# A two-layer hybrid decoder: first up tile with eight plain products, norm sums on VectorE, six banks for the output projection, another order of queues

## The chip, the cores and the metric

The kernel runs on one core of a Trainium2 chip. The metric is the device time of one execution in microseconds. The kernel before took 2763.81 us, the median of three runs (2761.84 to 2765.71).

The engines are named as the profile names them: PE is TensorE (matmuls), DVE is VectorE, ACT is ScalarE, POOL is GpSimd; SP issues most DMAs.

## The reference

One inference step over a prompt of 1024 tokens and eight sample sequences of 8 tokens with shared weights; the kernel treats them as 1088 columns of width 1024. Layer 0 mixes with an S5 state-space model, layer 1 with forgetting attention (FoX) over new and paged keys and values. Both have a cross-attention to a memory of 256 tokens and a squared-ReLU MLP of width 4096.

```
z = rmsnorm(h, norm_mix[i]) @ w_in[i]               # 768 main columns, 256 memory queries
y_mem = memory_attend(z[..., 768:], mem_k[i], mem_v[i])
layer 0: y = s5 scan of z (48 groups of 16 channels, 64 states)
         g = gelu(y);  y_main = g * sigmoid(g @ w_glu + b_glu)
layer 1: y_main = fox_attend(z, cumulative log-forget, past and new k, v)
h = h + concat(y_main, y_mem) @ w_out[i]
h = h + relu(rmsnorm(h, norm_mlp[i]) @ w_up[i])**2 @ w_down[i]
```

Outputs are the final norm of h, the S5 states, the memory and shared keys and values and the log-forget values, all float32.

## The kernel before

Every matmul operand is split into a rounded high part H and a rest L; a product is three matmuls (H·H, H·L, L·H; `mm3`, L209). The function `split` makes H on ScalarE (L221) and L, by a subtraction with two inputs, on an engine that is handed in (L222: VectorE, or GpSimd). The 1088 columns lie in four chunks of 272, and most matmuls are 128x272.

**S5 and GLU, layer 0.** The S5 work runs in units; GpSimd makes part of each (L1131, L1138, L1140, L1141), VectorE the rest (L1129, L1132, L1137), and a unit's result goes by ScalarE's queue (L1151) into the DRAM buffers yscr[0] to yscr[5]. SP loads them back in another layout (L1215), each is split for all four chunks, and only then the GLU's matmuls over six slices k can end. `past_rows` gathers past log-forget rows with 16 indirect DMAs on GpSimd (L1227), `past_sums` scans them on VectorE (L1233 to L1237) and stores them to fpast on SP (L1238). Their calls stand in the GLU's loop over chunks (c == 1, c == 3), but the scheduler puts instructions where it reckons that their engine is free, so they lie among the S5 units. Memory attention's 16 units are woven into the GLU's matmuls; their probabilities are scaled on GpSimd or VectorE (L734).

**Output projection and norm.** `out_proj` makes eight output tiles m for each chunk, first m = 0, 1 over all chunks, then m = 2 to 7 over all chunks, each tile of 24 matmuls in one of two PSUM banks (`dbank`); the addition to the residual (L329) frees it. When a chunk is whole, `mlp_norm` takes its sum of squares (`rms_sums`, L260, L261, on GpSimd; for the last chunk on VectorE), two ticks later its scale (L272 to L275), the product (L441; the last chunk L438, eight times), and then the MLP's operands.

**MLP up.** An up tile is a 2x2 block product in Winograd's form: seven block products instead of eight (`seven`), each of 12 matmuls per group of columns. Chunks 0 and 1 are group 0, chunks 2 and 3 are group 1; within a group the two chunks are the two column blocks. The form needs seven operands for a group of columns (`operands`: four split sums and differences, L356 to L363, and three plain ones) and seven for a tile of weights (`weight_ops`: four sums on GpSimd, L386 to L392, and seven splits). For the first tile (j = 14) group 0 and group 1 are made one after the other, and the weights' splits but the first lie on GpSimd; for the other 15 tiles both groups are made together and all splits lie on VectorE. Differences held back (`held`) and norms put off (`defer`, `tick`) come later in the program.

The order of instructions on each engine is set by a scheduler that reads the program in the order in which it is written, keeps data dependences and the edges of `issue_after` (`after(ins)`), and otherwise chooses by its own estimate of when things are ready.

## Time and profile before

| | us |
|---|---|
| median of three runs | 2763.81 |
| the profiled execution | 2768.41 |
| its span | 2766.5 |
| TensorE busy | 2569.8 (93%) |
| VectorE busy | 1963.9 (71%) |
| ScalarE busy | 1253.5 (45%) |
| GpSimd busy | 1310.3 (47%) |

The profile is of one execution; the row of the profiled execution is its whole time, the span is from its first to its last instruction. A timeline row gives the start, the duration, the engine, the line, the tile written and read, how many instructions it covers, and in brackets how long the engine was idle before it and what ended that. In a table by windows the count in brackets behind an engine's busy time is that of its instructions; PEclk is the granted clock of TensorE, 1.00 for 2.4 GHz and 0.50 for 1.2 GHz.

In time: S5 until about 298 us, GLU and memory attention until 410, output projection of layer 0 until 500, its MLP until 1235, layer 1's projections and attention until 1935, its output projection until 2020, its MLP to the end.

### The profile page before, as it was taken

What the parts mean: (1) busy time and instruction counts of PE and PEld (TensorE: products, weight loads), DVE (VectorE), ACT (ScalarE), POOL (GpSimd) and SP (SyncE); (2) the same over time, 40 slices, a digit from 0 to 9 for tenths busy, and PEclk for the clock granted to TensorE, in tenths of its full rate; (3) what the DMA queues carried; (4) which work ended last, traced back from release to release, by engine and by line L of the source; (5) the groups of instructions that cost most, each with busy time, mean ns of one, the idle gap of its engine ahead of it and who ended that gap; (6) DMA issues with size and microseconds to landing.
All of it is one profiled execution on the core that took longest, in us unless ns stands there. A gap on an engine that the chain in (4) does not pass through costs nothing.

```text
span 2766.5 us, 54068 instructions
## 1 busy us (share of the span) xinstructions
PE 2569.8 (93%) x20345; PEld 2401.5 (87%) x20345; DVE 1963.9 (71%) x3337; ACT 1253.5 (45%) x2592; POOL 1310.3 (47%) x1184
## 2 busy tenths in 40 slices
PE   6888799799998999999999999998979999899998
PEld 5877689799997999999889867776979999799998
DVE  8898654888886777784323278885488878577776
ACT  5433453566663222244322377774356666322224
...
GB/s 200 110 110 155 120 133 80 85 219 231 240 224 314 226 257 279 180 167 102 146 260 220 273 300 307 306 294 198 64 80 224 237 234 224 322 227 257 274 176 66
DMA packets 242283, 561.65 MB, mean 203 GB/s; under 512 B 54053, under 2 KB 129382, under 8 KB 224614
## 3 DMA queue, kind: packets, MB, share of 16 engines
...
q0 software_dynamic: 512, 0.79, 0.1%
...
## 4 chain that ended last, share of the span: by engine, by line
PE 44%; DVE 22%; DMA 13%; POOL 9%; issue 6%; ACT 5%; SPq 1%; POOLq 0%; ACTq 0%; DVEq 0%
PE banks L209 42%; DMA hops<-plain 7%; DVE rounded L222 6%; POOL plain L574 4%; DVE plain L222 3%; POOL plain L392 1%; ACT plain L221 1%; PE banks L1599 1%; DMA rounded<-hmid 1%; DVE plain L536 1%; POOL plain L582 1%; DMA hcnv<-plain 1%; ACT rounded L221 1%; POOL plain L388 1%; POOL plain L386 1%
## 5 line engine op out<-in xcount | busy, mean ns | idle before, releaser
L209 PE MATMUL banks<-rounded 128*128 128x272 f32 (+3 forms) x11168 | 1561.3, 296 | 108.6 <-ACT rounded L221 28.2
L209 PEld LDWEIGHTS banks<-rounded 128*128 128x128 f32 x11168 | 1465.6, 192 | 156.3 <-ACT rounded L221 31.9
L221 ACT ACTIVATE rounded<-plain 128x512 fp32r<-128x512 f32 (+5 forms) x571 | 379.8, 677 | 587.1 <-PE banks L209 420.9
L222 DVE TENSOR_TENSOR rounded<-plain,rounded 128x512 fp32r<-128x512 f32 (+4 forms) x500 | 509.0, 1022 | 119.8 <-ACT rounded L221 114.1
L209 PE MATMUL banks<-mlp,rounded 128*128 128x272 f32 x3840 | 524.1, 291 | 17.6 <-ACT rounded L221 11.1
L209 PEld LDWEIGHTS banks<-mlp,rounded 128*128 128x128 f32 x3840 | 499.9, 190 | 23.3 <-ACT rounded L221 12.3
L386 POOL TENSOR_TENSOR plain<-plain 128x512 f32<-128x512 f32 x60 | 91.5, 1525 | 488.9 <-DVE rounded L222 488.7
L574 POOL TENSOR_TENSOR plain<-plain,flex 128x544 f32<-128x544 f32 x192 | 290.8, 1523 | 42.3 <-DVE plain L573 39.8
L222 DVE TENSOR_TENSOR plain<-plain 128x544 fp32r<-128x544 f32 x212 | 165.0, 788 | 87.3 <-ACT plain L221 84.1
L221 ACT ACTIVATE plain<-plain 128x544 fp32r<-128x544 f32 x212 | 137.5, 649 | 145.1 <-DMA hops<-plain 123.5
L573 DVE TENSOR_TENSOR plain<-banks,plain 128x544 f32<-128x544 f32 x192 | 137.8, 718 | 54.7 <-PE banks L209 50.9
L392 POOL TENSOR_TENSOR plain<-plain 128x512 f32<-128x512 f32 x60 | 118.2, 1970 | 88.4 <-DVE rounded L222 87.9
L222 POOL TENSOR_TENSOR rounded<-plain,rounded 64x512 fp32r<-64x512 f32 (+4 forms) x71 | 112.0, 1586 | 76.9 <-ACT rounded L221 69.5
L537 ACT ACTIVATE plain<-plain 128x544 f32<-128x544 f32 (+1 forms) x136 | 85.3, 628 | 79.2 <-DVE plain L536 78.8
L209 PE MATMUL banks<-layer 128*32 128x256 f32 (+3 forms) x1152 | 111.8, 371 | 8.1 <-ACT layer L1422 3.9
L222 POOL TENSOR_TENSOR rounded<-flex,rounded 128x544 fp32r<-128x544 f32 (+7 forms) x100 | 67.3, 681 | 86.7 <-ACT rounded L221 74.0
L209 PE MATMUL banks<-flexr,rounded 128*128 128x272 f32 x768 | 108.3, 290 | 0.0
L209 PEld LDWEIGHTS banks<-flexr,rounded 128*128 128x128 f32 x768 | 101.9, 190 | 0.0
L536 DVE TENSOR_TENSOR plain<-banks,plain 128x544 f32<-128x544 f32 (+1 forms) x136 | 92.9, 683 | 5.3 <-PE banks L209 4.8
L221 ACT ACTIVATE rounded<-banks 128x512 fp32r<-128x512 f32 (+2 forms) x136 | 75.0, 559 | 46.4 <-PE banks L1599 32.7
L222 DVE TENSOR_TENSOR rounded<-banks,rounded 128x512 fp32r<-128x512 f32 (+2 forms) x136 | 85.9, 636 | 14.1 <-ACT rounded L221 12.2
L260 POOL TENSOR_TENSOR flex<-flex 128x544 f32<-128x544 f32 x18 | 27.6, 1533 | 138.9 <-ACT flex L258 90.9
...
## 6 DMA issues: line engine op xcount, KB each, us to landing
...
plain<-in_cache_kT SPq DMA_DIRECT2D x128, 384.0 KB
layer<-in_cache_v SPq DMA_DIRECT2D x128, 384.0 KB
...
```

The source lines that it names most:

```text
L209: PE.matmul(out, a, b, start=first, stop=last)
L221: S.activation(H, src, AF.Copy)
L222: e.tensor_tensor(L, src, H.bitcast(F32), op=ALU.subtract)
L386: G.tensor_tensor(a22, a21, a22, op=ALU.add)
L388: G.tensor_tensor(a11, a22, a11, op=ALU.subtract)
L392: G.tensor_tensor(a12, a12, a11, op=ALU.subtract)
L536: V.tensor_tensor(x, ps, u, op=ALU.add)
L537: S.activation(x, x, AF.Relu)
L573: V.tensor_tensor(h, ps, h, op=ALU.add)
L574: G.tensor_tensor(h, h, u, op=ALU.add)
L582: G.tensor_tensor(hc, hc, hr[:, m, :], op=ALU.add)
L1599: PE.transpose(tb[:, k, 128 * i:128 * i + 128], p[i][:, 2 * c + k, :], ident)
```

## The change

- First up tile, group 1: four output blocks as plain sums of two block products each (eight products, 96 matmuls, for seven, 84). Its operands for them are the plain halves of chunks 2 and 3; the first tile's weights get an eighth split (slot 7, `put(7, a21)`). The sums and differences of group 1 that the later tiles need are made afterwards (`held.pop()()`). The second up tile too is now made in two groups.
- `rms_sums` on VectorE for all chunks; the operand splits and the first weights' splits that lay on GpSimd go to VectorE.
- Output projection: six banks in turn. Tiles in the order m = 0, 1 for chunks 0 to 2; m = 2, 3 for chunk 0; m = 0, 1 for chunk 3; m = 4 to 7 for chunk 0; then m = 2 to 7 for chunks 1, 2, 3.
- Order: the loads of x, w_out and the page indices come behind the last yscr load on SP; the gathers behind the GLU's y sums of chunk 0 on GpSimd, the multiplication of the page indices beside them; the past sums behind VectorE's products of chunk 2; the hcnv stores in one order with the loads of `hops` (not shown).

The diff, cut to its core:

```diff
@@ -252,7 +252,7 @@
-    def rms_sums(h, w, e=G, ring=sq):
+    def rms_sums(h, w, e=V, ring=sq):
@@ -314,21 +314,40 @@
-    def out_proj(ys, w, hs, done):
+    def out_proj(ys, w, hs, done, ins=None):
...
-        def load(src, shape):
-            m, src = src
-            return wall(src, shape, to=more[2 * m - 12:2 * m - 10] if m > 5 else None)
...
-        for g, n in ((0, 2), (2, 6)):
-            def ev(i, c, ps, w_, g=g):
-                r = hs[c][:, g + i, :]
-                V.tensor_tensor(r, ps, r, op=ALU.add)
...
-            dense([(m, w[m]) for m in range(g, g + n)], ys, ev, load, done=(lambda c: done(hs[c], c)) if g else None)
+        obank = Banks([0, 1, 2, 3, 4, 5])
+        W = {}
...
+        def load(ms):
+            with after(ins):
+                for m in ms:
+                    W[m] = wall(w[m], [128, 8, 128], to=more[2 * m - 12:2 * m - 10] if m > 5 else None)
...
+        def tiles(ms, c):
+            (xH, xL), n = ys[c], CH[c][1]
+            for m in ms:
+                H, L = W[m]
+                ps = obank([128, 512])
+                for k in range(8):
+                    mm3(ps[:, :n], H[:, k, :], L[:, k, :], xH[:, k, :], xL[:, k, :], k == 0, k == 7)
+                r = hs[c][:, m, :]
+                V.tensor_tensor(r, ps[:, :n], r, op=ALU.add)
+                tick()
...
+        load(range(4))
+        for c in range(3):
+            tiles((0, 1), c)
+        tiles((2, 3), 0)
+        tiles((0, 1), 3)
+        load(range(4, 8))
+        tiles(range(4, 8), 0)
+        done(hs[0], 0)
+        for c in range(1, NC):
+            tiles(range(2, 8), c)
+            done(hs[c], c)
@@ -346,7 +365,7 @@
-    def operands(b11, b12, b21, b22, extra, put, which=(0, 1, 2, 6)):
+    def operands(b11, b12, b21, b22, extra, put, which=(0, 1, 2, 5, 6)):
@@ -359,7 +378,8 @@
-            put(5, b22)
+            if 5 in which:
+                put(5, b22)
@@ -367,7 +387,7 @@
-    def weight_ops(src, cells, sh, e=V):
+    def weight_ops(src, cells, sh, more=None):
@@ -379,10 +399,13 @@
         def put(i, x):
-            split(r[i][:, 0], r[i][:, 1], x, e if i else V)
+            split(r[i][:, 0], r[i][:, 1], x)
...
         put(6, a22)
+        if more:
+            r.append(wr[more].at([128, 2, *sh], F32R))
+            put(7, a21)
@@ -427,7 +450,7 @@
-        s1 = rms_sums(h, w, V if last else G)
+        s1 = rms_sums(h, w)
@@ -449,23 +472,22 @@
-            extra = (nt0, setA[1])[g].at([128, 4, w]) if c % 2 else None
...
-            def put_of(g):
-                def put(i, t):
-                    o = xop(i, g)
-                    split(o[:, 0], o[:, 1], t, G if i in (2, 6) and not last else V)
-                return put
+            def put(i, t):
+                o = xop(i, g)
+                split(o[:, 0], o[:, 1], t)
...
-                operands(*b, extra, put_of(g), (0, 2))
+                operands(*b, None, put, (0, 2))
             elif not last:
-                operands(*b, extra, put_of(g), (1,))
-                held.append(lambda: operands(*b, extra, put_of(g), (6,)))
+                operands(*b, nt0.at([128, 4, w]), put, (1, 5))
+                held.append(lambda: operands(*b, None, put, (6,)))
             else:
                 held.pop()()
-                operands(*b, extra, put_of(g), (1, 6))
+                put(6, b[1])
+                put(5, b[3])
+                held.append(lambda: operands(*b, setA[0].at([128, 4, w]), put, (1, 6)))
@@ -474,12 +496,21 @@
-        def up_weights(j, e=V):
+        def up_weights(j, more=None):
-                              lambda r: (r[:, 0, 0:4], r[:, 0, 4:8], r[:, 1, 0:4], r[:, 1, 4:8]), [4, 128], e)
+                              lambda r: (r[:, 0, 0:4], r[:, 0, 4:8], r[:, 1, 0:4], r[:, 1, 4:8]), [4, 128], more)
@@ -524,13 +546,17 @@
-        W = up_weights(14, G)
+        assert turn["w"] % 3 == 0
+        W = up_weights(14, 7)
...
-            for gs in (slice(0, 1), slice(1, 2)) if n == 0 else (slice(0, 2),):
+            for gs in (slice(0, 1), slice(1, 2)) if n < 2 else (slice(0, 2),):
+                if n == 0 and gs.start:
+                    continue
...
                 def out(m, n, ps, u):
@@ -539,8 +565,20 @@
-                if gs.stop == 1:
-                    flush()
+            if n == 0:
...
+                flush()
+                for m, c in ((1, 0), (0, 0), (1, 1), (0, 1)):
+                    turn["bank"] = (turn["bank"] + 1) % 3
+                    ps = banks[:, 1024 * turn["bank"]:1024 * turn["bank"] + CN]
+                    for i in range(2):
+                        a, x = W[((0, 2), (7, 6))[m][i]], xop(((0, 2), (6, 5))[c][i], 1)
+                        for k in range(4):
+                            mm3(ps, a[:, 0, k, :], a[:, 1, k, :], x[:, 0, k, :], x[:, 1, k, :], i + k == 0, i + k == 4)
+                    t = q[m][c][:, 1]
+                    S.activation(t, ps, AF.Relu)
+                    S.activation(t, t, AF.Square)
+                held.pop()()
@@ -1212,17 +1250,18 @@
-        SY.dma_start(out=zs, in_=yscr[q].rearrange("(t c) g j -> (c g) t j", c=16))
+        zi = SY.dma_start(out=zs, in_=yscr[q].rearrange("(t c) g j -> (c g) t j", c=16))
...
-    SY.dma_start(out=pidx, in_=I["page_rows"])
-    SY.dma_start(out=hrow, in_=I["head_rows"])
-    V.tensor_scalar(pidx, pidx, 12.0, hrow[:, 0:1], op0=ALU.mult, op1=ALU.add)
+    with after(zi):
+        SY.dma_start(out=pidx, in_=I["page_rows"])
+        SY.dma_start(out=hrow, in_=I["head_rows"])
...
     def past_rows():
+        G.tensor_scalar(pidx, pidx, 12.0, hrow[:, 0:1], op0=ALU.mult, op1=ALU.add)
@@ -1240,9 +1279,11 @@
         if c == 1:
-            past_rows()
+            with after(gi):
+                past_rows()
         if c == 3:
-            past_sums()
+            with after(vi):
+                past_sums()
@@ -1254,8 +1295,8 @@
-            G.tensor_tensor(y, xH[:, m, :].bitcast(F32), xL[:, m, :].bitcast(F32), op=ALU.add)
-            V.scalar_tensor_tensor(y, t, 1.0, y, op0=ALU.add, op1=ALU.mult)
+            gi = G.tensor_tensor(y, xH[:, m, :].bitcast(F32), xL[:, m, :].bitcast(F32), op=ALU.add)
+            vi = V.scalar_tensor_tensor(y, t, 1.0, y, op0=ALU.add, op1=ALU.mult)
@@ -1267,10 +1308,10 @@
-    hs = [load_x(c) for c in range(NC)]
+    hs = [load_x(c, zi) for c in range(NC)]
         load_ym(0, c, 208 if c == NC - 1 else None)
-    out_proj(yx, I["w_out"][0], hs, lambda h, c: mlp_norm(h, c, 2))
+    out_proj(yx, I["w_out"][0], hs, lambda h, c: mlp_norm(h, c, 2), zi)
```

On SP's queue, from the last but one yscr load to the last, before:

```order
L1215 DMA plain<-yscr_135 128x8x136
L1209 DMA plain<-in_w_glu 128x768 x5
L1238 DMA fpast<-plain 96x1024 x2
L671 DMA plain<-in_cmk 128x512
L1190 DMA out_s5f<-prep_150 128x432
L671 DMA plain<-in_cmk 128x512
L197 DMA plain<-in_w_out 128x1024
L1215 DMA plain<-yscr_136 128x8x136
```

There the fpast stores (L1238), waiting for past sums, have ten later transfers behind them. After:

```order
L1253 DMA plain<-yscr_135 128x8x136
L694 DMA plain<-qmscr_86 128x2x64
L1253 DMA plain<-yscr_136 128x8x136
L1259 DMA plain<-in_page_rows 96x16
L1228 DMA out_s5f<-prep_150 128x432
L1260 DMA plain<-in_head_rows 96x1
L197 DMA plain<-in_w_out 128x1024
```

The last yscr load (yscr_136) moved ahead of the memory cache, w_out and the fpast stores.

On GpSimd's queue, the last S5 unit and the GLU's first y sums (L1257, after L1298; L1131 is L1169 after, L1138 is L1176), before:

```order
L1227 DMA plain<-in_logf_rows,plain 96x128 x4
L1131 TENSOR_TENSOR plain<-plain 128x512
L1138 TENSOR_TENSOR flex_69<-plain 64x2x128 x2
L1140 TENSOR_TENSOR prep_150<-plain 128x2
L1141 TENSOR_TENSOR prep_150<-plain 128x2
L1257 TENSOR_TENSOR plain<-rounded 128x272 x2
```

The last unit's first sum (L1131) has four gathers ahead of it. After:

```order
L1179 TENSOR_TENSOR prep_150<-plain 128x2
L1169 TENSOR_TENSOR plain<-plain 128x512
L1176 TENSOR_TENSOR flex_69<-plain 64x2x128 x2
L1178 TENSOR_TENSOR prep_150<-plain 128x2
L1179 TENSOR_TENSOR prep_150<-plain 128x2
L222 TENSOR_TENSOR rounded<-plain,rounded 128x768 x2
L1298 TENSOR_TENSOR plain<-rounded 128x272 x2
```

There the two last units follow each other, and no gather stands between.

On VectorE at the end of layer 0's output projection, from the last addition (L337) to the second tile, after (L434, L438, L442 and L562 take products out of PSUM, L375 to L383 are the differences):

```order
L337 TENSOR_TENSOR plain<-banks,plain 128x272
L222 TENSOR_TENSOR rounded<-plain,rounded 128x512
L275 TENSOR_TENSOR flex_69<-flex_69 128x272
L260 TENSOR_TENSOR flex_69<-flex_69 128x544
L464 TENSOR_TENSOR plain<-plain,flex_69 128x2176
L562 TENSOR_TENSOR plain<-banks,plain 128x272
L261 TENSOR_TENSOR flex_69<-flex_69 128x272
L434 TENSOR_TENSOR plain<-banks,plain 128x272
L438 TENSOR_TENSOR plain<-banks,plain 128x272
L562 TENSOR_TENSOR plain<-banks,plain 128x272 x2
L442 TENSOR_TENSOR plain<-banks,plain 128x272
```

These are the last addition, chunk 2's product and the first products of the tile. The next on VectorE, with chunk 3's norm:

```order
L222 TENSOR_TENSOR rounded<-plain,rounded 128x1088
L272 TENSOR_TENSOR flex_69<-flex_69 128x272
L562 TENSOR_TENSOR plain<-banks,plain 128x272
L222 TENSOR_TENSOR rounded<-plain,rounded 128x1088
L273 SCALAR_TENSOR_TENSOR flex_69<-banks,flex_69 128x272
L274 TENSOR_SCALAR flex_69<-flex_69 128x272
L275 TENSOR_TENSOR flex_69<-flex_69 128x272
L461 SCALAR_TENSOR_TENSOR plain<-plain,flex_69 128x272 x8
L375 TENSOR_TENSOR plain<-plain 128x1088
L222 TENSOR_TENSOR flexr_4581<-plain,flexr_4581 128x1088
L376 TENSOR_TENSOR plain<-plain 128x1088
L222 TENSOR_TENSOR flexr_4580<-plain,flexr_4580 128x1088
```

The second split into flexr ends the operands of the first tile; L379, two splits of 128x1088 and the first split of the second tile's weights follow. Before, from chunk 3's norm on:

```order
L272 TENSOR_TENSOR flex_69<-flex_69 128x272
L273 SCALAR_TENSOR_TENSOR flex_69<-banks,flex_69 128x272
L274 TENSOR_SCALAR flex_69<-flex_69 128x272
L275 TENSOR_TENSOR flex_69<-flex_69 128x272
L438 SCALAR_TENSOR_TENSOR plain<-plain,flex_69 128x272 x8
L536 TENSOR_TENSOR plain<-banks,plain 128x272
L222 TENSOR_TENSOR rounded<-plain,rounded 128x512
L356 TENSOR_TENSOR plain<-plain 128x1088
L222 TENSOR_TENSOR flexr_4578<-plain,flexr_4578 128x1088
L357 TENSOR_TENSOR plain<-plain 128x1088
L360 TENSOR_TENSOR plain<-plain 128x1088
L222 TENSOR_TENSOR rounded<-plain,rounded 128x1088 x2
```

Before, the differences L356 to L363 and the splits of what they give stood ahead of the first tile's later products; now, two splits into flexr suffice for its plain products.

On TensorE, from the last output tile to the first tile's chunk 3 products (operand flexr), after:

```order
L209 MATMUL banks<-rounded,mlp_3589 128x272 x24
L209 MATMUL banks<-mlp_3586,rounded 128x272 x12
L209 MATMUL banks<-rounded 128x272 x3
L209 MATMUL banks<-mlp_3587,rounded 128x272 x2
L209 MATMUL banks<-rounded 128x272 x9
L209 MATMUL banks<-mlp_3587,rounded 128x272 x10
L209 MATMUL banks<-rounded 128x272 x24
L209 MATMUL banks<-flex_69,plain 128x272
L209 MATMUL banks<-rounded 128x272 x12
L209 MATMUL banks<-mlp_3588,rounded 128x272 x12
L209 MATMUL banks<-rounded 128x272 x48
L209 MATMUL banks<-flexr_4581,rounded 128x272 x13
```

And before:

```order
L209 MATMUL banks<-mlp_3586,rounded 128x272 x3
L209 MATMUL banks<-rounded 128x272 x12
L209 MATMUL banks<-mlp_3587,rounded 128x272 x12
L209 MATMUL banks<-rounded 128x272 x45
L209 MATMUL banks<-flex_69,plain 128x272
L209 MATMUL banks<-rounded 128x272 x3
L209 MATMUL banks<-mlp_3588,rounded 128x272 x12
L209 MATMUL banks<-rounded 128x272 x12
L209 MATMUL banks<-mlp_3586,rounded 128x272 x12
L209 MATMUL banks<-rounded 128x272 x12
L209 MATMUL banks<-flexr_4578,rounded 128x272
```

After, 132 matmuls of the first tile stand between the last output tile and the first that reads flexr; before, about as many (123 of them shown) stood there.

## Rows read from the trace of the kernel before

**Rows 1.** The page's first part: busy us, share and instructions of each engine.

```profile
PE 2569.8 (93%) x20345; PEld 2401.5 (87%) x20345; DVE 1963.9 (71%) x3337; ACT 1253.5 (45%) x2592; POOL 1310.3 (47%) x1184
```

**Rows 2.** By windows: stretch, its us; busy (instructions) by engine; PEclk; DMA share; GB/s.

```profile
290.00:295.00 5.00, 0.00 (x0) 0.00 (x0) 0.96 (x1) 0.84 (x1) 3.48 (x5) 0.50 0.89 291
...
2010.00:2015.00 5.00, 5.00 (x42) 5.00 (x41) 5.00 (x5) 1.90 (x3) 4.92 (x4) 1.00 0.01 3
...
480.00:540.00 60.00, 43.19 (x294) 40.21 (x293) 52.09 (x61) 29.04 (x52) 39.57 (x18) 0.91 0.14 49
...
2005.00:2060.00 55.00, 39.80 (x267) 37.73 (x266) 48.78 (x56) 26.59 (x46) 38.34 (x17) 0.92 0.12 45
```

**Rows 3.** Timeline of SP's queue, 225 to 300: start, us, engine, operation, [idle <-releaser].

```profile
269.18 0.38 SPq L1215 DMA_DIRECT2D plain<-yscr  x1
...
286.03 1.01 SPq L1238 DMA_DIRECT2D fpast<-plain  x2
...
290.13 0.42 SPq L1215 DMA_DIRECT2D plain<-yscr  x1
```

**Rows 4.** GpSimd: the gathers as a group (busy, mean ns | idle <-), and its timeline.

```profile
L1227 POOL DMA_INDIRECT plain<-in_logf_rows,plain x16 | 17.7, 1104 | 4.0 <-issue 2.9 <-PE banks L209 0.5 <-DVE rounded L222 0.3
...
267.61 1.29 POOL L1131 TENSOR_TENSOR plain<-plain 128x512 f32<-128x512 f32 x1
```

**Rows 5.** Timeline of VectorE, 240 to 300.

```profile
245.14 0.69 DVE L1121 TENSOR_TENSOR plain<-banks,plain 128x508 f32<-128x508 f32 x1 [2.09 <-POOL flex L1138]
...
263.67 0.69 DVE L1132 TENSOR_TENSOR plain<-plain 128x512 f32<-128x512 f32 x1
...
272.13 1.32 DVE L1137 TENSOR_TENSOR flex<-plain 64x256 f32<-64x256 f32 x2
...
273.48 2.75 DVE L1233 TENSOR_TENSOR_SCAN plain<-plain 96x1024 f32<-96x1024 f32 x1
```

**Rows 6.** Timeline of ScalarE and its queue, 270 to 300.

```profile
273.15 2.12 ACT L221 ACTIVATE rounded<-plain 128x272 fp32r<-128x272 f32 x5 [3.90 <-DMA plain<-yscr]
...
277.34 0.33 ACTq L1151 DMA_DIRECT2D yscr<-flex  x1
```

**Rows 7.** Timeline of TensorE: GLU, end of memory attention, MLP's start in layer 0.

```profile
297.83 2.47 PE L209 MATMUL banks<-rounded 128*128 128x272 f32 x7 [12.21 <-ACT rounded L221]
...
404.45 0.66 PE L209 MATMUL banks<-glu 128*64 128x128 f32 x8 [0.95 <-DVE glu L741]
...
408.60 0.53 PE L209 MATMUL banks<-rounded 128*128 128x272 f32 x2 [2.32 <-ACT rounded L221]
...
499.56 1.75 PE L209 MATMUL banks<-rounded 128*128 128x272 f32 x12 [3.03 <-DVE plain L329]
...
520.61 1.83 PE L209 MATMUL banks<-rounded 128*128 128x272 f32 x10 [3.85 <-DVE rounded L222]
...
534.72 0.82 PE L209 MATMUL banks<-mlp,rounded 128*128 128x272 f32 x2 [5.07 <-ACT rounded L221]
```

**Rows 8.** Timeline of VectorE at the MLP's start in layer 0.

```profile
489.36 1.81 DVE L260 TENSOR_TENSOR flex<-flex 128x544 f32<-128x544 f32 x1
...
493.95 3.40 DVE L441 TENSOR_TENSOR plain<-plain,flex 128x2176 f32<-128x2176 f32 x1
...
516.21 3.39 DVE L438 SCALAR_TENSOR_TENSOR plain<-plain,flex 128x272 f32<-128x272 f32 x8
...
519.87 0.68 DVE L222 TENSOR_TENSOR rounded<-plain,rounded 128x512 fp32r<-128x512 f32 x1
...
521.67 1.29 DVE L222 TENSOR_TENSOR flexr<-plain,flexr 128x1088 fp32r<-128x1088 f32 x1
...
534.81 0.72 DVE L222 TENSOR_TENSOR plain<-plain 128x544 fp32r<-128x544 f32 x1
```

**Rows 9.** Timeline of GpSimd there.

```profile
495.04 3.45 POOL L392 TENSOR_TENSOR plain<-plain 128x512 f32<-128x512 f32 x1
...
520.69 9.41 POOL L392 TENSOR_TENSOR plain<-plain 128x512 f32<-128x512 f32 x1 [5.16 <-DVE rounded L222]
```

18 lines of the change are left out of this document (9 added, 9 removed).

## The prediction

> **What bounds the kernel now.** The page's busy times come first: TensorE is busy 2569.8 of 2766.5 us, so only some 197 us of the span can be won without taking matmuls away [rows 1]. The table by windows then says where TensorE stands still. At full clock 42 of the kernel's 128x272 matmuls fill 5.00 us, 0.119 us each; in 290 to 295 none ran; and in the two stretches in which a layer's output projection gives way to its MLP there are 294 matmuls in 60 us and 267 in 55 us [rows 2]. At 0.119 us these are 35.0 and 31.8 us of work, so 25 and 23 us are lost, 48 in both layers. These two places and the start of the GLU are what the change touches; the body of the MLP, the attention and the down projection keep their order.
>
> At the start of the GLU the reader follows one transfer back. TensorE resumes at 297.83 after 12.21 us, on a ScalarE split [rows 7] of the last yscr load, which SP issued at 290.13, behind the fpast stores at 286.03 [rows 3]. These wait for the scan of past sums that VectorE began at 273.48 [rows 5]. The data of that load had been sent off at 277.34 [rows 6]. So two delays stand one behind the other: the last S5 unit is late, and its load is queued late.
>
> At the MLP's start TensorE waits 3.03 us for an output-projection addition (two PSUM banks), 3.85 for a VectorE split, 5.07 for a ScalarE split [rows 7]. The last follows a GpSimd sum of 9.41 us at 520.69 [rows 9], during which VectorE works through chunk 3's norm and differences.
>
> **Part 1, S5 to GLU.** The 16 row gathers leave GpSimd's S5 stretch: 17.7 us and 4.0 us idle around them [rows 4]. What of it was on the path: VectorE stood 2.09 us for GpSimd at 245.14; in the last unit its sum was done at 264.36, yet GpSimd's L1131 began at 267.61, after four gathers, 3.25 us; then L1137 began at 272.13, behind splits of yscr, though L1131, on which it rests, had ended at 268.90, some 3 us [rows 4, 5]. With one scan of about 2.5 us moved out of VectorE's way this is 2.1 + 3.3 + 3 + 2.5 = 11, so the last write leaves at about 266 instead of 277.34. From such a write to the load's landing I take 4 us for the write (an estimate: as long as a load) and 4.0 us for the load (269.18 to ScalarE's 273.15 [rows 3, 6]); with two splits of below 0.5 us TensorE has its last operand near 277 to 282. If the unit stays where it is and only the queue is mended, it is 277.34 + 8 = 286. Gain 12 to 21 us; I take 16.
>
> **Part 2, what the gathers meet now.** They stand in GpSimd's queue in GLU chunk 1, behind the y sums, and memory attention's scaling of probabilities is queued behind them: about 20 us of its engine, while the attention units feed on the same GLU matmuls as filler. By the order 7 of 16 units are through when the GLU ends, 10 before, so nine stand in the tail with little beside them. Before, the tail's waits were 0.95 and 2.32 us [rows 7]; three more units at up to 2.3 us and a fall of the clock make up to 12 us, and nothing if the tail's units overlap each other. I take 6. The past sums now lie on VectorE in chunk 3 of the GLU (5 us of scans), where it is not late; that costs nothing unless the fpast stores hold up w_out on SP. The page-index loads and multiplication stand right before the gathers and hold nobody else. Parts 1 and 2: gain 10, between 0 and 21.
>
> **Part 3, the MLP's start, per layer.** Added: 12 matmuls (eight products for seven in one group), 12 x 0.119 = 1.4 us, on the path whenever TensorE is. Moved to VectorE: nine 128x544 sums and three 128x272 sums of the norms, three operand splits of 128x1088, six weight splits; added: one weight split and one operand split. What decides is one list, VectorE's, from the last addition of the output projection to the first chunk 3 operand. In the changed order that is 22 operations of 128x272, 0.42 each by the eight that take 3.39: 9.3 us; one 128x512 split, 0.68; one 128x544 sum; the 128x2176 product, 3.40; four of 128x1088, 1.29 each, 5.2 [rows 8]. The sum of 128x544 is 0.72 if it costs what the split of that size does and 1.81 beside a busy GpSimd [rows 8]. Together 19.3 to 20.4 us. TensorE's cover, by the order, is 132 matmuls (group 0's seven products and chunk 2's half of the plain ones), 15.7 us. So it waits some 4 us there, since it needs two splits of chunk 3 and no difference; before, the differences stood in front, and it waited 3.85 and 5.07 [rows 7]. Then come 48 matmuls, 5.7 us, beside which VectorE still does 7.1 us (five of 128x1088, one 0.68): 1.4 us of wait. Then the second tile begins while VectorE has, by the order, thirteen rows of splits, differences and additions, 12.3 us at the same prices, beside some 9 us of matmuls: 3.3 us. In all 38.7 us of list against 30.4 of cover: 8 us with everything at its quiet price. VectorE's operations beside GpSimd took up to 1.81/0.72 times as long [rows 8]; GpSimd keeps about eight weight sums here, and I allow 6 us for that as the upper end: 8 to 14, I take 11, and 1 for what six banks leave of the 3.03. So of 24 us lost, 12 stay, less 1.4: **gain about 10 us a layer**, 20 in both. Ends: with no contention and the clock held, 24 - 5 - 1.4 = 17; with the list stretched until the wait is what it was, -2.
>
> The held differences (four of 128x1088 and four splits) come behind the plain products; their cover is the second tile's group 0, and where it is gone their 10 us would be waited for. Since the splits of 128x512 on GpSimd are gone, its sums begin at once. The hcnv stores are tied to the loads' order at the end of the up projection, where SP is not waited for: nothing.
>
> One row speaks against putting two-input work on VectorE: GpSimd's L392, 3.45 us at 495.04, took 9.41 at 520.69 while VectorE ran two-input operations without a break [rows 9]. The Trainium skill, GPSIMD Engine Reference, "Key points", says that GpSimd shares its SBUF interfaces with VectorE and contends with VectorE instructions that have two SBUF inputs. By that rule the sums left on GpSimd stay long; the sum above has them short. The trace agrees that the two slow each other; how much is left when GpSimd does four sums and no splits, no run here shows.
>
> **Sum.** 10 + 20 = 30 us. The profiled execution took 2768.4 us (span 2766.5), 4.6 above the median of 2763.8, and would become 2738; on the median, **2734**.
>
> **Rivals.** (a) *VectorE is the new bound.* For it: its list is already longer than its cover. At 1.35 times the quiet price the list is 52 us, the wait 22, and with 1 and 1.4 the loss is 24 as before: Part 3 gives nothing, 2763.8 - 10 = 2754. Against it: GpSimd loses most of its work there, so it slows VectorE less than before.
> (b) *Memory attention pays for Part 1.* Tail 12, start 12: 20 remain, 2744. For it: half of GpSimd's tail is now closer to TensorE; against: before, most units had cover to spare.
> (c) *The sharing stays.* The 9.41 us sum remains on the path in both layers; against 2 to 3 us that is 7 a layer: 2734 + 14 = 2748. Its rule is the one named above.
> (d) *Slower.* The same list, from the last output-projection addition into the second tile, at 1.7 times, about half way from quiet to the 2.5 times of 1.81 for 0.72: 65.8 us against 30.4 of cover, a wait of 35; with 1 and 1.4 it is 37 for 24, +13 a layer, less 10 from Parts 1 and 2: 2780. It decides from about 1.5 times.
> (e) *Part 1 isn't had*: something else, a GLU weight or the chunk's other operands, is late at 297: 20 - 6 = 14, 2750.
>
> **How the numbers follow.** Forecast 0.46, (a) 0.15, (b) 0.13, (c) 0.12, (d) 0.09, (e) 0.05. A measurement can tell about 0.2% here, 5.5 us: faster means below 2758.3. Forecast, (b), (c) and (e) are faster, 0.76, of which 0.02 may come out the same; (a) lies near the edge, 0.08 faster, 0.06 the same, 0.01 slower; (d) is slower, 0.09. Faster 0.82, same 0.08, slower 0.10. Low end: Part 1 at 18 net and 17 a layer, 52, 2712; high end: (a) with the list at 1.42 times, 2 x 3 more, 2760.
>
> **What would show it.** Right: TensorE's first steady GLU matmul near 280; the last yscr load issued right behind its write; windows of 60 us at the MLP's start with some 80 matmuls more; waits there below 5 us each. Wrong: attention waits over 10 us in sum before 410 (Part 2), a GpSimd sum of 9 us before the MLP's second tile (c), VectorE's list from the last output addition to chunk 3's first operand at 30 us or more (d).

## The result and the profile after

The changed kernel takes 2732.68 us (median of four runs, 2728.14 to 2739.15); the kernel before took 2764.76 us beside it (four runs, 2761.84 to 2768.74). The ratio is 0.9885, with an interval of 0.9861 to 0.9909. The forecast was 2734. The time was met, and the terms of its sum were not: one of its two gains is a loss, and about as much was won at two places that the sum had at nothing. The rest of this text is on that.

The page's first part, of the changed kernel:

```profile
PE 2563.4 (94%) x20369; PEld 2393.5 (88%) x20369; DVE 1969.2 (72%) x3382; ACT 1259.1 (46%) x2612; POOL 1226.7 (45%) x1143
```

Windows of 60 us at the MLP's starts, of the changed kernel (columns as in [rows 2]):

```profile
480.00:540.00 60.00, 53.61 (x401) 52.07 (x399) 55.10 (x75) 37.35 (x66) 11.73 (x6) 0.97 0.19 70
...
1970.00:2030.00 60.00, 53.89 (x393) 52.40 (x392) 56.56 (x73) 38.61 (x67) 12.36 (x7) 0.94 0.18 65
```

Against [rows 1, 2]: TensorE runs 24 matmuls more, and the windows hold 401 and 393 matmuls where those of before held 294 in 60 us and 267 in 55 us. The forecast had some 80 more in 60 us; it is 107 in layer 0. But windows at two places do not add up to a time, since the stages lie elsewhere in the two kernels. For that, the matmuls finished since the start are counted: for a time in the profile of before, the table has the time at which the changed kernel had finished as many (by windows from 0, interpolated over 2 us). The difference is its lead.

| before, us | matmuls | changed kernel, us | lead | what lies ahead of it |
|---|---|---|---|---|
| 300 | 1685 | 286.7 | 13.3 | start of the GLU |
| 320 | 1826 | 320.2 | -0.2 | the gathers |
| 420 | 2595 | 429.1 | -9.1 | GLU, memory attention |
| 560 | 3519 | 560.9 | -0.9 | MLP start, layer 0 |
| 850 | 5815 | 850.0 | 0.0 | MLP up |
| 900 | 6055 | 889.8 | 10.2 | up to down, layer 0 |
| 1300 | 9092 | 1290.0 | 10.0 | MLP down, layer 1's input |
| 1900 | 14033 | 1882.9 | 17.1 | layer 1's attention |
| 1940 | 14311 | 1912.5 | 27.5 | its output projection begins |
| 2000 | 14785 | 1972.4 | 27.6 | output projection |
| 2080 | 15244 | 2045.5 | 34.5 | MLP start, layer 1 |
| 2380 | 17623 | 2345.8 | 34.2 | MLP up |
| 2420 | 17799 | 2377.5 | 42.5 | up to down, layer 1 |

The 12 added matmuls of a layer count as lead here, 1.4 us each time, from 560 and from 2080 on. The two spans differ by 40.2 us, the medians by 32: the profiled execution of before lies 4.6 us above its first median, and that of the changed kernel, 2728.14, is its fastest run.

### The profile page after: what moved, and what is told of

The parts are those of the page before. It is cut to its first block, busy times and chain, and to the rows that moved or that the text cites. A ratio compares the mean times of both kernels' runs of the same rounds, so it can differ in the third digit from the quotient of the medians.

```text
span 2726.3 us, 54081 instructions
## 1 busy us (share of the span) xinstructions
PE 2563.4 (94%) x20369; PEld 2393.5 (88%) x20369; DVE 1969.2 (72%) x3382; ACT 1259.1 (46%) x2612; POOL 1226.7 (45%) x1143
## 4 chain that ended last, share of the span: by engine, by line
PE 46%; DVE 23%; DMA 12%; POOL 8%; issue 6%; ACT 5%; SPq 0%; POOLq 0%; ACTq 0%; DVEq 0%
PE banks L209 43%; DMA hops<-plain 7%; DVE rounded L222 6%; POOL plain L612 4%; DVE plain L222 3%; PE banks L1640 1%; ACT plain L221 1%; DMA rounded<-hmid 1%; POOL plain L620 1%; DVE plain L562 1%; ACT rounded L221 1%; POOL plain L409 1%; DMA flex<-ymscr 1%; POOL plain L415 1%; POOL plain L410 1%
## 5 line engine op out<-in xcount | busy, mean ns | idle before, releaser
L222 DVE TENSOR_TENSOR rounded<-plain,rounded 128x512 fp32r<-128x512 f32 (+4 forms) x518 | 518.7, 1007 | 107.9 <-ACT rounded L221 103.0
L209 PE MATMUL banks<-mlp,rounded 128*128 128x272 f32 x3816 | 517.3, 290 | 7.7 <-DVE rounded L222 2.1
L209 PEld LDWEIGHTS banks<-mlp,rounded 128*128 128x128 f32 x3816 | 493.8, 189 | 12.4 <-DVE rounded L222 4.2
L409 POOL TENSOR_TENSOR plain<-plain 128x512 f32<-128x512 f32 x60 | 96.9, 1615 | 707.4 <-DVE rounded L222 707.4
L415 POOL TENSOR_TENSOR plain<-plain 128x512 f32<-128x512 f32 x60 | 99.7, 1662 | 62.0 <-DVE rounded L222 61.5
L209 PE MATMUL banks<-flexr,rounded 128*128 128x272 f32 x816 | 117.8, 295 | 5.6 <-ACT flexr L221 4.0
L209 PEld LDWEIGHTS banks<-flexr,rounded 128*128 128x128 f32 x816 | 110.7, 195 | 6.5 <-ACT flexr L221 4.4
L222 POOL TENSOR_TENSOR rounded<-plain,rounded 64x512 fp32r<-64x512 f32 (+2 forms) x55 | 78.4, 1434 | 67.6 <-ACT rounded L221 62.3
L222 DVE TENSOR_TENSOR rounded<-banks,rounded 128x512 fp32r<-128x512 f32 (+2 forms) x136 | 86.0, 637 | 13.7 <-ACT rounded L221 11.8
L562 DVE TENSOR_TENSOR plain<-banks,plain 128x544 f32<-128x544 f32 (+1 forms) x136 | 90.4, 666 | 5.0 <-PE banks L209 4.6
L209 PE MATMUL banks<-rounded,layer 128*128 128x256 f32 x480 | 89.8, 300 | 2.7 <-ACT rounded L221 2.5
```

The lines of the kernel that those rows point to most:

```text
L209: PE.matmul(out, a, b, start=first, stop=last)
L222: e.tensor_tensor(L, src, H.bitcast(F32), op=ALU.subtract)
L409: G.tensor_tensor(a22, a21, a22, op=ALU.add)
L415: G.tensor_tensor(a12, a12, a11, op=ALU.subtract)
L562: V.tensor_tensor(x, ps, u, op=ALU.add)
```

## Experiments

Each run starts from the changed kernel where nothing else is said. Ratios are to the kernel before, on the same chip; the changed kernel's own is 0.9885.

### The stores of the last up tile

```diff
-                        load_on(to[:, i, :, n], t[:, i].bitcast(F32))
+                        SY.dma_start(out=to[:, i, :, n], in_=t[:, i].bitcast(F32))
```

> The changed kernel with one edit undone: the hcnv stores of the last up tile are issued again without an edge to the loads' order. The prediction put this edit at nothing: then the time is the changed kernel's, 2733 within 5 us. The rival from the two traces: before, VectorE waited 4.47 us for hcnv stores and TensorE 8.60 us (layer 0) and 8.19 us (layer 1) for VectorE's L571 at the first down tile, and the changed kernel has neither wait; then undoing costs 15 to 19 us, 2748 to 2752, and the two waits of over 8 us are back, with eight hcnv stores spread over some 19 us.

2752.21 us, ratio 0.9953 (0.9937 to 0.9969): 19.5 us are lost. By the lead, 9.1 of them go between 850 and 900 us (it goes from 0.5 to 1.6, in the changed kernel from 0.0 to 10.2) and 8.9 between 2380 and 2420. Timeline of TensorE at the first down tiles of layers 0 and 1, the kernel before (columns as in [rows 3]):

```profile
884.58 5.80 PE L209 MATMUL banks<-rounded 128*128 128x272 f32 x24 [8.60 <-DVE plain L571]
...
2405.55 4.89 PE L209 MATMUL banks<-rounded 128*128 128x272 f32 x24 [8.19 <-DVE plain L571]
```

SP's queue in layer 0 at that place, the kernel before:

```profile
854.70 1.06 SPq L515 DMA_DIRECT2D mlp<-hops  x2
...
860.72 2.95 SPq L515 DMA_DIRECT2D rounded<-hops  x2
...
867.98 19.31 SPq L501 DMA_DIRECT2D hcnv<-plain  x8
```

VectorE there, and one window (columns as in [rows 2]), the kernel before:

```profile
883.80 1.36 DVE L571 TENSOR_TENSOR plain<-banks,flex 128x544 f32<-128x544 f32 x2 [4.47 <-DMA hcnv<-plain]
...
865.00:885.00 20.00, 8.11 (x38) 7.27 (x39) 8.00 (x9) 3.75 (x6) 4.18 (x3) 0.70 1.03 407
```

TensorE at the first down tiles, the run with free stores:

```profile
885.34 4.91 PE L209 MATMUL banks<-rounded 128*128 128x272 f32 x24 [8.18 <-DVE plain L609]
...
2387.84 4.63 PE L209 MATMUL banks<-rounded 128*128 128x272 f32 x24 [7.32 <-DVE plain L609]
```

SP's queue, the run with free stores:

```profile
868.73 19.39 SPq L532 DMA_DIRECT2D hcnv<-plain  x8
```

SP's queue, the changed kernel:

```profile
870.61 6.36 SPq L513 DMA_DIRECT2D hcnv<-plain  x8
877.06 1.28 SPq L513 DMA_DIRECT2D mlp<-hops  x2
878.39 1.16 SPq L513 DMA_DIRECT2D rounded<-hops  x2
```

TensorE at layer 1's first down tile, the changed kernel:

```profile
2367.72 3.26 PE L209 MATMUL banks<-rounded 128*128 128x272 f32 x24 [1.03 <-DVE plain L609]
```

In the kernel before and in the run with free stores, eight hcnv stores stretch over more than 19 us and TensorE waits 7 to 9 us in each layer for VectorE's addition; in the changed kernel they are out in 6.36 us, and of the wait 1.03 us is left in layer 1 and none in layer 0. VectorE had itself waited 4.47 us before for hcnv stores to leave its buffers (there are three, `hl`, for four splits). What the edge changes on SP's queue is what stands ahead of the stores: before, four loads of the next operands (mlp<-hops and rounded<-hops, two each, 1088 KB each by the page's list of DMA issues) were issued ahead of them, and from 865 to 885 us the DMA engines were busy throughout (share 1.03; in the changed kernel 1.00); in the changed kernel the same four come behind the stores, 18 to 22 us later. The run with free stores has the order of before, the run below that of the changed kernel, in both layers. So the stores, and with them the buffers, waited behind loads that could go later. This is read from the order and the windows; no run moves these loads alone. The prediction said of this edit: "where SP is not waited for: nothing". This is the wrong term.

The same edit alone, on the kernel before:

> The kernel before with one part of the change alone: the hcnv stores tied into the loads' order. The prediction: nothing, 2765. By the run with this edit undone (19.5 us slower than the changed kernel) it gives 15 to 20 us by itself, 2745 to 2750, and the waits of 8.60 and 8.19 us at the first down tile are gone; less, if it needs the rest of the change.

2748.14 us, ratio 0.994 (0.9918 to 0.9961), 16.6 us by the ratio and 19.4 by the medians; the lead goes from -1.2 at 850 us to 9.0 at 900 and from 10.5 at 2380 to 19.2 at 2420. Of the waits of 8.60 and 8.19 us, 1.31 and 2.70 are left. It needs nothing else of the change.

### Six banks

```diff
-        obank = Banks([0, 1, 2, 3, 4, 5])
+        obank = Banks([0, 1])
```

> The changed kernel with two PSUM banks in the output projection instead of six, its new order of tiles kept. The prediction gave the six banks some 2 us a layer at the MLP's start: 2737. The rival from the traces: in layer 1 the six banks let TensorE pass a residual chunk that lands late (7.90 us of wait for the addition L329 at 1934.76 before, none after), so two banks cost about 8 us there and 2 to 3 at each MLP start: about 2746, with a wait of 6 to 8 us for an addition at the start of layer 1's output projection.

2748.4 us, ratio 0.9937 (0.9914 to 0.996): 15.7 us by the medians, 14 by the ratios. By the lead, 9.1 us of it go between 1900 and 1940 (from 7.2 to 8.5, in the changed kernel from 17.1 to 27.5), 1.7 between 420 and 560 (from -14.5 to -8.0, against -9.1 to -0.9) and 1.2 between 2000 and 2080. Another 5.4 us are gone at 420 already, ahead of the first output projection, where this execution's memory attention ends 6 us later; that the banks do this is not shown. TensorE at the start of layer 1's output projection, the kernel before:

```profile
1934.76 19.84 PE L209 MATMUL banks<-rounded 128*128 128x272 f32 x144 [7.90 <-DVE plain L329]
```

VectorE there, the kernel before:

```profile
1934.17 0.79 DVE L329 TENSOR_TENSOR plain<-banks,plain 128x272 f32<-128x272 f32 x2 [3.02 <-DMA plain<-hscr]
```

TensorE there, and at the MLP's start of layer 0, the run with two banks:

```profile
530.11 0.82 PE L209 MATMUL banks<-flexr,rounded 128*128 128x272 f32 x2 [4.86 <-ACT flexr L221]
...
1927.99 19.67 PE L209 MATMUL banks<-rounded 128*128 128x272 f32 x144 [7.75 <-DVE plain L337]
```

VectorE there, the changed kernel:

```profile
1914.69 0.44 DVE L337 TENSOR_TENSOR plain<-banks,plain 128x272 f32<-128x272 f32 x1 [0.51 <-DMA plain<-hscr]
```

The addition waits for a residual chunk (hscr) that lands late; with two banks the next tile waits with it, 7.75 us with two banks and 7.90 before. In the changed kernel the addition at 1914.69 waits for its chunk too, and TensorE has no such wait there, since its next tile has another bank. The prediction gave six banks 2 us a layer, at the MLP's start alone; there the 1.7 and 1.2 us bear it out. Chunk 3's operand is waited for 4.86 us with two banks and 2.00 in the changed kernel; why, no run tells. What the prediction left out is the start of layer 1's output projection.

### The MLP's start

The functions `rms_sums`, `operands`, `weight_ops`, `mlp_norm` and the first two up tiles are those of before, the rest is the changed kernel's:

```diff
-        W = up_weights(14, 7)
+        W = up_weights(14, G)
...
-            for gs in (slice(0, 1), slice(1, 2)) if n < 2 else (slice(0, 2),):
+            for gs in (slice(0, 1), slice(1, 2)) if n == 0 else (slice(0, 2),):
```

> The changed kernel with the MLP's start as before: norm sums of three chunks and part of the splits on GpSimd, first up tile by seven products in both groups, second tile with both groups together. The prediction gave this part 10 us a layer: 2753. The count of matmuls over time gives 7.7 in layer 0 and 6.7 in layer 1: 2747. If six banks alone do it, nothing is lost: 2733.

2742.53 us, ratio 0.9915 (0.9892 to 0.9939): 9.9 us for both layers by the medians, 8 by the ratios. By the lead it is 5.4 us in layer 0 (420 to 560) and 8.6 in layer 1 (2000 to 2080), less 1.4 of added matmuls each: 11. The forecast's 20 was for this and six banks' share there, some 3 us by the run with two banks; so the place is worth 12 to 14, about two thirds of what was forecast.

What the list was to be can be read directly. VectorE in the changed kernel, layer 0, from the last output addition to the second operand of chunk 3:

```profile
504.80 0.43 DVE L337 TENSOR_TENSOR plain<-banks,plain 128x272 f32<-128x272 f32 x1
...
506.10 0.71 DVE L260 TENSOR_TENSOR flex<-flex 128x544 f32<-128x544 f32 x1
...
506.74 2.41 DVE L464 TENSOR_TENSOR plain<-plain,flex 128x2176 f32<-128x2176 f32 x1
...
525.85 1.28 DVE L222 TENSOR_TENSOR flexr<-plain,flexr 128x1088 fp32r<-128x1088 f32 x1
```

TensorE at chunk 3's two operands and in the second tile, the changed kernel:

```profile
523.45 0.52 PE L209 MATMUL banks<-flexr,rounded 128*128 128x272 f32 x2 [2.00 <-ACT flexr L221]
...
524.78 7.46 PE L209 MATMUL banks<-flexr,rounded 128*128 128x272 f32 x46 [0.81 <-DVE flexr L222]
...
540.46 0.77 PE L209 MATMUL banks<-rounded 128*128 128x272 f32 x4 [2.08 <-ACT rounded L221]
```

Two windows of that stretch (columns as in [rows 2]), the changed kernel:

```profile
525.00:530.00 5.00, 5.00 (x30) 5.00 (x31) 5.00 (x5) 3.78 (x5) 0.00 (x0) 0.70 0.00 0
...
540.00:545.00 5.00, 4.06 (x18) 3.84 (x19) 4.56 (x5) 3.48 (x7) 4.92 (x4) 0.66 0.46 156
```

From 504.80 until the first operand, 524.72, are 19.9 us; the sum was 19.3 to 20.4. The 128x544 addition cost 0.71 us, the lower of the two bounds. That the sum fits is in part luck: the 128x2176 product took 2.41 us for the 3.40 in the sum, and 2.6 us of the stretch are VectorE's own waits for TensorE and ScalarE, which the sum did not have. TensorE waited 2.00 and 0.81 us there, and 1.58 and 0.32 ahead of it: 4.7 for the 4 predicted. In the second tile its five waits sum to 4.5 us (2.08, 0.48, 0.46, 0.81, 0.66) for 4.7. So the waits are right to 0.7 us and better. What the sum lacked is the clock: after the waits TensorE ran at 0.96 and 0.70 in 520 to 530, part of it at the lower of its two levels, and 30 matmuls filled 5.00 us where 42 do at full clock; after the wait of 2.08 us it ran at 0.66 in 540 to 545, and 18 matmuls took 4.06 us where 34 would fit. At 0.119 us for each matmul that is missing this is 3.3 us in layer 0, an estimate.

The norm sums alone, put back on GpSimd:

```diff
-    def rms_sums(h, w, e=V, ring=sq):
+    def rms_sums(h, w, e=G, ring=sq):
...
-        s1 = rms_sums(h, w)
+        s1 = rms_sums(h, w, V if last else G)
```

> The changed kernel with the norm's sums of squares of chunks 0 to 2 on GpSimd again (the last chunk's on VectorE, as before); all else of the MLP's start is kept. The prediction saw VectorE's list as what bounds the MLP's start: of its sums only one 128x544 stands in the list behind the last addition, so little changes there; on VectorE the others lie beside output-projection matmuls: 2733 within 5. If the two engines' contention is what counts, GpSimd's sums slow VectorE's list and it is 5 to 10 us slower: 2738 to 2743. If VectorE is overloaded by the sums, it is faster, 2725.

2732.28 us, ratio 0.9878 (0.9861 to 0.9894): no change. Where these sums lie is of no account to the time, as the list said: one of them stands in it.

### The gathers and the GLU's start

```diff
-    with after(zi):
-        SY.dma_start(out=pidx, in_=I["page_rows"])
-        SY.dma_start(out=hrow, in_=I["head_rows"])
+    SY.dma_start(out=pidx, in_=I["page_rows"])
+    SY.dma_start(out=hrow, in_=I["head_rows"])
+    V.tensor_scalar(pidx, pidx, 12.0, hrow[:, 0:1], op0=ALU.mult, op1=ALU.add)
...
-            with after(gi):
-                past_rows()
+            past_rows()
```

> The changed kernel with the page-index loads, their multiplication on VectorE and the 16 gathers free to go where the kernel before had them, among the S5 units; the past sums stay in the GLU's chunk 3, the yscr loads stay ahead. The prediction counts the move as a gain: without it the last S5 unit is late again by about 10 us and memory attention is early by 6: 2735 to 2740. The rival from the count of matmuls over time (changed kernel 9 us ahead at 300 us, 12 us behind at 420): in the GLU the gathers cost more than they gave, 8 us of TensorE waits beside them and about as much in memory attention's tail, so putting them back gains: 2718 to 2728, without waits of TensorE that have no visible cause between 300 and 316.

2722.67 us, ratio 0.9844 (0.9824 to 0.9864): 10 us faster than the changed kernel. The move of the gathers, which the prediction counted as a gain, is a loss. With them in the GLU, spread out:

```diff
+            if c and 6 * c + m < 22:
+                with after(gi):
+                    past_rows([6 * c + m - 6])
```

> The changed kernel with its 16 gathers in the GLU not as one burst but one behind each y sum of chunks 1 to 3, and the past sums behind the last tile of chunk 3. Theory 1: the burst holds memory attention's scaling on GpSimd for 20 us; spread out, the tail's loss goes, about 10 us: 2722. Theory 2: the gathers as such disturb TensorE (waits without a visible cause, 6.9 us between 302 and 313 in the changed kernel); then those waits remain, only spread, and the time is 2726 to 2733. Theory 3: neither matters, 2733.

2726.31 us, ratio 0.985 (0.983 to 0.9869): 6 us faster by the medians, with intervals that overlap a little. The waits without a cause are gone, not spread, so neither theory has it whole. And without gathers:

```diff
-        for i in range(16):
-            G.indirect_dma_start(out=fp[i // 8][:, 128 * (i % 8):128 * (i % 8) + 128], out_offset=None,
...
+        for i in range(2):
+            SY.dma_start(out=fp[i].rearrange("p (k n) -> p k n", k=8),
```

> The changed kernel with the gathers left out: two plain loads on SP of fixed rows take their place, so the past log-forget rows are the wrong ones. It measures what the gathers cost in all. If the burst in the GLU costs what the count of matmuls shows between 300 and 420 us (some 20 us, of which 7 to 8 in waits without a visible cause), the time is 2710 to 2715, and those waits are gone. If the loss there has another cause, memory attention's new place in the order, it is 2725 to 2733.

2719.57 us, ratio 0.9839 (0.9823 to 0.9856), between the two that were expected. The gathers cost 13 us in the GLU; among the S5 units it is 3 us by the medians and 1 by the ratios, which is not clear of the intervals. GpSimd's gathers as a group in the changed kernel (busy us, mean ns | idle us before them):

```profile
L1266 POOL DMA_INDIRECT plain<-in_logf_rows,plain x16 | 15.6, 978 | 4.7 <-issue 4.7
```

TensorE beside them, and then in memory attention's tail, the changed kernel:

```profile
306.68 3.29 PE L209 MATMUL banks<-rounded 128*128 128x272 f32 x14 [4.20 <-issue]
...
312.46 0.28 PE L209 MATMUL banks<-rounded 128*128 128x272 f32 x1 [1.58 <-issue]
...
315.21 9.10 PE L209 MATMUL banks<-rounded 128*128 128x272 f32 x54 [1.45 <-ACT flex L1297]
...
387.88 1.92 PE L775 MATMUL banks<-plain,glu 128*128 128x128 f32 x8 [2.06 <-DVE rounded L222]
```

TensorE at the burst in the run with norm sums on GpSimd, whose gathers are the same:

```profile
306.37 10.85 PE L209 MATMUL banks<-rounded 128*128 128x272 f32 x72 [1.27 <-ACT flex L1297]
```

ScalarE in the changed kernel, then ScalarE and TensorE in the run with free stores:

```profile
306.14 0.49 ACT L1297 ACTIVATE flex<-banks,plain 128x272 f32<-128x272 f32 x1 [0.75 <-remote]
...
315.74 0.49 ACT L1297 ACTIVATE flex<-banks,plain 128x272 f32<-128x272 f32 x1 [9.42 <-issue]
...
316.28 9.76 PE L209 MATMUL banks<-rounded 128*128 128x272 f32 x54 [5.78 <-issue]
```

"Issue" is time in which the engine waited for nothing that the profile shows, "remote" time that ended with a signal whose sender it does not name. In the changed kernel 6.9 us of TensorE's waits between 302 and 313 are of the first kind, in the run with free stores 8.4, with the old MLP start 6.3, with two banks 2.6 (and 9.90 us for ScalarE behind them); in the run with norm sums on GpSimd none, though it has the same gathers. Without gathers, with spread ones and with those among the S5 units there is at most 0.3. In the run with three buffers, below, where the burst is broken off once, there are none either. So the waits come with the burst, in four of six profiles. The longest of them end 0.05 us behind ScalarE's L1297, which empties a GLU tile's bank (306.14 and 0.49 against 306.68, 315.74 and 0.49 against 316.28), so there TensorE may have waited for ScalarE, as it did in the run with norm sums on GpSimd by its row. But ScalarE had waited too, without a cause that a row names; and the changed kernel's waits of 0.41, 1.58 and 0.43 us lie inside one tile of 18 matmuls. What is lacking in them stays open.

The count says where the rest goes. The lead over the kernel before:

| | 300 | 320 | 420 | transposes, first to last |
|---|---|---|---|---|
| kernel before | 0 | 0 | 0 | 309.5 to 406.0 |
| changed kernel | 13.3 | -0.2 | -9.1 | 301.4 to 413.8 |
| norm sums on GpSimd | 11.8 | 6.8 | -5.1 | 303.3 to 407.6 |
| gathers spread | 11.3 | 6.6 | -1.5 | 303.8 to 410.0 |
| no gathers | 11.2 | 9.4 | 0.5 | 303.6 to 404.7 |
| gathers among S5 | 5.7 | 4.2 | 5.6 | 300.9 to 402.8 |
| past sums there too | 0.9 | -2.7 | -5.2 | 314.1 to 412.0 |

Between 300 and 320 the burst takes 13.5 us with these waits and, in the run with norm sums on GpSimd, 5.0 without them; the medians of the two kernels are the same, so the waits are not shown to be worth anything in the median. From 320 to 420 the changed kernel loses 8.9 us, and the run without any gathers loses 8.9 as well: this part is not the gathers' doing. The stretch from 300 to 410 us of the kernel before, the changed kernel, the one without gathers and the one with the gathers among the S5 units (columns as in [rows 2]):

```profile
300.00:410.00 110.00, 105.32 (x842) 94.15 (x841) 72.00 (x149) 60.41 (x171) 25.31 (x32) 0.98 0.37 113
...
300.00:410.00 110.00, 93.51 (x697) 79.19 (x695) 65.69 (x135) 51.68 (x149) 29.78 (x36) 0.94 0.37 117
...
300.00:410.00 110.00, 99.77 (x771) 86.72 (x770) 71.12 (x146) 59.14 (x166) 24.18 (x28) 0.94 0.37 117
...
300.00:410.00 110.00, 105.29 (x857) 94.24 (x857) 71.66 (x146) 57.86 (x160) 24.01 (x26) 1.00 0.40 123
```

TensorE stands 4.7 us there before, 16.5 in the changed kernel, 10.2 without gathers and 4.7 with the gathers among the S5 units, and the granted clock is 0.98, 0.94, 0.94 and 1.00. Memory attention's transposes of probabilities, the last column of the table, show what it is. A row is the group of its 64 matmuls, with minimum, median and maximum in ns, and the start of the first and of the last. The kernel before:

```profile
L737 PE MATMUL banks<-plain,glu x64: 270/272/328, 309.5 to 406.0; 128*128 128x128 f32 x64
```

The changed kernel:

```profile
L775 PE MATMUL banks<-plain,glu x64: 270/273/445, 301.4 to 413.8; 128*128 128x128 f32 x64
```

Without gathers:

```profile
L775 PE MATMUL banks<-plain,glu x64: 270/272/421, 303.6 to 404.7; 128*128 128x128 f32 x64
```

With the gathers among the S5 units:

```profile
L775 PE MATMUL banks<-plain,glu x64: 270/272/329, 300.9 to 402.8; 128*128 128x128 f32 x64
```

With the past sums among them too (the run of the next section):

```profile
L775 PE MATMUL banks<-plain,glu x64: 270/272/473, 314.1 to 412.0; 128*128 128x128 f32 x64
```

From first to last they take 96.5 us before, 101.1 without gathers, 101.9 with the gathers among the S5 units, 97.9 with the past sums there too, and 112.4 in the changed kernel; in every run with gathers in the GLU, spread or not, it is 104 to 114. So the chain has a length of its own, longer beside the gathers, and its end moves with its start. The lead at 420 follows that end to within 4 us in each row (a chain that ends 7.8 us later than before, a lead of -9.1; 3.2 earlier, 5.6), and not the lead at 300. A GLU that begins 11 to 13 us earlier, with a chain that begins only 6 to 8 us earlier and takes longer, uses up the matmuls that were to fill under it, and TensorE then waits at a lower clock. The prediction saw this tail as a price of the gathers (6 us, 12 at most); by these rows it is the bound of the stage, though no run moves the chain alone.

### The sums, and the buffers before the GLU

The run with the gathers among the S5 units, and the past sums free too:

```diff
-            with after(vi):
-                past_sums()
+            past_sums()
```

> The run with the gathers back among the S5 units, and now the past sums free as well, as the kernel before had them. The prediction's steps: one scan of 2.5 us on VectorE's way and the fpast stores ahead of the last yscr load on SP, so the GLU starts later by the wait of that load behind the stores, 5 to 8 us: 2728 to 2731. Rival: the GLU's start is held by other loads (the wait of 9.93 us for ScalarE in the run before was for a memory-key split, and its last yscr load was issued at 286.29 anyway): 2723, no change against that run.

2726.82 us, ratio 0.9856 (0.9836 to 0.9876): 4 us slower than with the sums in the GLU by the medians, though the intervals overlap. The lead at 300 us falls from 5.7 to 0.9, as the step on the fpast stores says. These stores hold up more than the yscr load: SP's load of the memory keys (glu<-mkscr) goes out at 294.03 for 284.11, and memory attention's transposes begin at 314.1 for 300.9.

ScalarE's queue at the last yscr write, in the changed kernel:

```profile
267.31 0.33 ACTq L1189 DMA_DIRECT2D yscr<-flex  x1
```

SP's queue, the last two yscr loads:

```profile
277.23 0.37 SPq L1253 DMA_DIRECT2D plain<-yscr  x1
...
280.28 0.38 SPq L1253 DMA_DIRECT2D plain<-yscr  x1
```

VectorE, splits of the loaded slices:

```profile
264.53 4.36 DVE L222 TENSOR_TENSOR rounded<-plain,rounded 128x272 fp32r<-128x272 f32 x2 [2.04 <-ACT rounded L221]
...
273.45 5.36 DVE L222 TENSOR_TENSOR rounded<-plain,rounded 128x272 fp32r<-128x272 f32 x7
```

The write left at 267.31; 266 was predicted. Its load should have gone out 4 us later and went out at 280.28. The two buffers of the ring were taken: their splits, 0.42 us each when VectorE is alone, took 4.36 us for two while GpSimd split GLU weights, and 5.36 for seven, in most of which it made y sums. A third buffer:

```diff
-    zring = ga.sub(0, 2176).ring(2, 1088)
+    zring = ga.sub(0, 3264).ring(3, 1088)
```

> The changed kernel with three buffers instead of two for the yscr loads before the GLU. In the changed kernel the last yscr data left at 267.31, as predicted (266), yet its load was issued only at 280.28: the ring's two buffers were held by VectorE's splits. If that ring is what the prediction missed, the last load goes out 8 to 10 us earlier and TensorE's steady GLU begins 5 to 8 us earlier: 2725 to 2728. If VectorE's list of splits itself is the bound (it was busy from 264 to 281), a third buffer gives 0 to 2 us: 2731 to 2733.

2740.0 us, ratio 0.9891 (0.9864 to 0.9918): nothing gained, and above what either view expected. But the scheduler also put the S5 units in another order with it: the last write left at 271.74, the last load at 283.08. So it does not tell whether the ring or VectorE's splits held the load, and this stays open. With the gathers among the S5 units:

> The run with the gathers back among the S5 units, with three buffers for the yscr loads. There TensorE waited 9.93 us at 291.13, in which the last yscr load was issued at 286.29, behind a transfer of memory keys. If the ring held it, the wait falls by 5 us or more: 2715 to 2718; if it is the memory keys' own chain, nothing: 2723.

2713.83 us, ratio 0.9806 (0.9787 to 0.9824), the fastest version here, 1.9% below the kernel before. TensorE at the GLU's start in the run with two buffers:

```profile
291.13 3.32 PE L209 MATMUL banks<-glu 128*128 128x512 f32 x6 [9.93 <-ACT glu L221]
```

In the run with three:

```profile
288.68 9.05 PE L209 MATMUL banks<-rounded 128*128 128x272 f32 x42 [3.32 <-ACT rounded L221]
```

With the third buffer the wait is 3.32 us, for a yscr split, where it was 9.93 for a split of the memory keys; the last yscr load went out at 283.33 for 286.29, and the lead at 300 is 8.9 us for 5.7. But the lead at 420 is 6.5 us for 5.6: memory attention's chain again (last transposes at 401.9 for 402.8), so the third buffer's 9 us in the medians are not shown to come from there. The intervals of the two ratios touch at 0.9824.

## Why the prediction was right or wrong

| term | predicted | by the count | by undoing it |
|---|---|---|---|
| Parts 1 and 2, GLU | +10 | -9.1 | |
| - the gathers' move in it | a gain | | -10 |
| Part 3, both MLP starts | +20 | 12.3 net | 9.9, and six banks' share of 3 |
| six banks, layer 1's output projection | 0 | 10.4 | 9.1 of 15.7 |
| the stores' order | 0 | 18.5 | 19.5 |
| layer 1's attention | 0 | 7 | |

*What bounds the kernel now.* The step named three places where TensorE stands still, and left out three waits of about 8 us that are as plain in the timeline of before: 8.60 us at 884.58, 8.19 at 2405.55, 7.90 at 1934.76. It went by the places that the change was thought to touch, not by the list of TensorE's waits. The last row of the table, between 1300 and 1900 us, where the order is that of before, is not explained; the runs with gathers among the S5 units, and with the stores alone, have 3 us there.

*Part 1.* The late last unit was read rightly (266 for 267.31). The step that failed is the next one, from the write to the load: the load was taken to wait for the data alone, and went out 13 us behind the write. TensorE's matmuls are steady from 285 to 287 us on, where 277 to 282 was forecast. The lead at 300 us, 13.3, is still within its 12 to 21.

*Part 2.* This is the step that failed most: the term of 6 us measured 22.4, between 300 and 420. Its mechanism, the burst, accounts for about half: the run without gathers loses 10.7 us there all the same. The rest is put down to the chain of memory attention, whose end moves with its own start; a GLU that starts earlier was counted as gain in full, and that is the overlap that the sum had wrong. Its sign of being wrong, attention waits over 10 us in sum, came: 16.5 us between 300 and 410. Rival (b) named the tail and put it at 12. Rival (e), a GLU that starts no earlier, did not come: the start was had, and was worth nothing at the stage's end.

*Part 3.* The list, the cover and the waits came out near what was worked, the list in part by luck. The gain of 10 a layer is 6.8 and 5.5 by the count. The step that was mis-sized is TensorE behind its waits, priced at full clock; the lower clock cost some 3.3 us in layer 0 by the estimate above. The gain was taken from 24 us lost, in which the slow clock and the output projection's own additions were contained.

*The rule on the two engines' shared interfaces, rival (c).* The trace agrees that the two slow each other, at another place. Timeline of GpSimd in the second tile, the changed kernel:

```profile
534.42 5.32 POOL L409 TENSOR_TENSOR plain<-plain 128x512 f32<-128x512 f32 x1 [33.76 <-DVE rounded L222]
...
539.82 1.29 POOL L410 TENSOR_TENSOR plain<-plain 128x512 f32<-128x512 f32 x1
```

VectorE there, the changed kernel:

```profile
543.30 1.77 DVE L222 TENSOR_TENSOR rounded<-plain,rounded 128x512 fp32r<-128x512 f32 x1
```

A weight sum took 5.32 us beside VectorE's two-input splits (the one of the same size behind it 1.29), and a 128x512 split 1.77 us for 0.68. The waits of the second tile were priced without this, so their fit is luck too. The Trainium skill, GPSIMD Engine Reference, "Key points", names contention of GpSimd with VectorE instructions that have two SBUF inputs. On the first tile's list it had no weight, since GpSimd stood idle there until 534.42, where a VectorE split released it; the prediction had its sums "begin at once". So rivals (a), (c) and (d), which all rest on it, did not come, for a reason that the prediction had not given.

*The sum.* 2734 for 2732.7 is errors that cancel: 19 us too much for the GLU and some 8 for the MLP's starts, against 29 us for the banks and the stores and 7 in layer 1's attention that the sum had at nothing. That is 9 us more than the forecast's 30 by the count of two executions, of which the medians show 2.
